# A two-layer encoder trunk: the small matmuls of attention gathered into fewer bursts, weights made ready a unit ahead

## The chip, the cores and the metric

The kernel runs on one core of a Trainium2 chip. The metric is the device time of one execution in microseconds (us); lower is better. Five engines work side by side: TensorE (PE in the profile; its weight loads are PEld), VectorE (DVE), ScalarE (ACT), GpSimd (POOL) and SyncE (SP), which here issues most of the DMA transfers.

## The reference

512 tokens of width 1024 go through two layers, each an attention and a SwiGLU network (width 2816), with RMSNorm ahead of each and at the end. Everything is float32.

```python
for i in range(DEPTH):
    h = rmsnorm(x, norm_mix[i])
    if i % 2 == 0: x = x + window_gqa_sink(h, w_qkv_a[j], w_out_a[j], sink_a[j])
    else:          x = x + dilated_mixture_attention(h, w_qkv_b[j], w_out_b[j])
    x = x + swiglu(rmsnorm(x, norm_ffn[i]), w_gate[i], w_up[i], w_down[i])
return rmsnorm(x, norm_final)
```

Layer 0's attention: 16 query heads of 64, 4 key and value heads, a token sees 128 tokens to each side, with a linear distance bias and a learned sink logit. Layer 1's: three groups of 16 heads, each with queries, keys and values of its own: (window 128, dilation 1), (512, 4), (2048, 16). A dilated group sees only the tokens of its own residue class. The three outputs of a head are merged with weights from the softmax denominators:

```python
for gi, (win, dil) in enumerate(DILATED_GROUPS):
    ...
    o, lse = banded_attention(q, k, v, slopes, dil, win // (2 * dil), BLOCK_B)
wts = jax.nn.softmax(jnp.stack(lses), axis=0)
o = jnp.einsum('gbsh,gbshd->bshd', wts, jnp.stack(outs))
```

## The kernel before

**Projections.** A weight block of 1024x128 is a *unit*: it is loaded (`wraw`, by SyncE), split by ScalarE into a high part `wh` and by VectorE into a low part `wl` (`split`, L93 and L94), and multiplied in three products per 128 rows (`mm3`, L122): high by high, high by low, low by high, each in two matmuls of 256 columns. The buffers for `wraw`, `wh` and `wl` number three each. `unit` is a generator with 8 steps of six matmuls; `values` makes the values of four heads out of two weight blocks in 16 steps of six matmuls. When a unit's last matmul is issued, its `done` is called: for a query or key unit of layer 1 VectorE scales the result out of PSUM (L980, L991).

**The order on TensorE is written by hand**; the other engines' instructions are put in order by a planner. The small matmuls of attention are the main thread and the projection steps are *fillers* between them, so that TensorE has work while ScalarE and VectorE are at the softmax. `spread([a, 3, b], fill)` runs `a`, then three filler steps, then `b`; `weave(steps, fill, total)` spreads `total` filler steps over the steps of a list.

**Layer 1, a pair of heads at a time (8 pairs).** Its parts, with what they are called in the profile:

- `scores_a` (L1036, tile `sc`): scores of group 0, two tiles at a time; VectorE adds the bias and takes the maximum (L1044), ScalarE the exponential (L1049). Queries and keys of group 0 are used in split form: `split_keys` (called in `k_done`) writes the tiles `ks` and `kl` from the key unit's result with four copies on ScalarE for the high parts (L136, L137), two subtractions on VectorE (L138) and two copies of the low parts on ScalarE (L139).
- `merge`: the maxima and denominators of group 0 go by GpSimd's DMAs (L1165, L1166, L1171) through DRAM into another order of tokens (`sa`).
- `turn_a` (L1058, tile `tp`): transposes of the probabilities; `weigh_a` (L1073, L1077, tile `ov`): their products with the values, taken over by ScalarE into `acca` (L1082).
- `scores_b` (L1095): scores of the two dilated groups, for two of four classes at a time; maximum on VectorE (L1108), minimum with group 0's (L1111), exponential on ScalarE (L1115), the sum of all three groups (L1118 to L1120), then the probabilities are scaled on ScalarE (L1127).
- `turn_b` (L1137 on TensorE, L1140 on VectorE): transposes; `merge_rows` (L1177): group 0's weights, multiplied into `acca` (L1179).
- `weigh_b` (L1150, tile `ov`): products with the dilated values, added to `acca` (L1156) and split into `oh`, `ol` (L93, L94).

`scores_b` uses 64 of the 128 rows of TensorE's array per matmul, two matmuls side by side; `weigh_a` and `weigh_b`, like `weigh` of layer 0 (L394), use 64 columns each.

`attention_a` lists the first three of these groups and `attention_b` the last three. The fillers of a pair p are its dilated query and key units, values where they are due, the query and key unit of group 0 for pair p+1, and at the end parts of the output projection (`out_part`).

**Layer 0.** 16 units of attention (four groups of heads by four blocks of 128 queries). Each has scores (L144), softmax on VectorE and ScalarE, scaling on GpSimd (L373), transposes `turn` (L380, evacuated at L384 and L386), and `weigh` (L394), whose result ScalarE and VectorE split into `oh` and `ol` (L398, L399). `weigh` of one unit stands after the first `turn` of the next, and the scores run two units ahead.

PSUM has eight banks: three with the tag `mm`, two `sc`, two `tp`, one `ov`.

Of the kernel before, what the change touches and what calls it, by code (L numbers as in the profile page):

```python
# [16 lines left out]
NK = D // 128  # L17
# [49 lines left out]
def trunk(ctx, tc, xT, gains, sink, tabs, qsc, wunits, wv, outT, outR):  # L67
# [81 lines left out]
    def run(gen):  # L149
        for _ in gen:  # L150
            pass
# [19 lines left out]
                for _ in range(step):  # L171
                    next(fill)

    def unit(u, hi, lo, tag, done, cuts=(0, NK)):


        def gen():
            tiles = weight_tiles()
            wh, wl = chunks(tiles, (NK, 128))
            ps = bank(tag)  # L180
            for j in range(NK):
                if j in cuts:
# [10 lines left out]
    def values(i, col, hi, lo, out, tags="mm mm mm mm"):  # L193


        def gen():
            w = [load_unit(wv[2 * i + k], (4, 256), 96, 1 + (i == 0 and k == 0)) for k in range(2)]
            for b in range(4):
# [112 lines left out]
    with tc.tile_pool(name="l0", bufs=2) as pool:  # L311
# [26 lines left out]
        def attention0(P, h, b):  # L338
# [37 lines left out]
            def turn(kb):  # L376
                tp = bank("tp")
                for hf in range(2):
                    for i in range(2):
                        nc.tensor.transpose(tp[:, 256 * hf + 128 * i:256 * hf + 128 * i + 128],  # L380
                                            st["pr"][:, 2 * i + hf, 128 * kb:128 * kb + 128], ident)
                pt = st["pt", kb] = pool.tile([128, 512], F32, name="pt", bufs=4)
# [5 lines left out]
            def weigh():  # L388

                ov = bank("ov")  # L390
                for kb in range(nb):
                    for hf in range(2):
                        vs = slice(64 * (2 * P + hf), 64 * (2 * P + hf) + 64)
                        nc.tensor.matmul(ov[64 * hf:64 * hf + 64, :256], v0[:, k0 // 128 + kb, vs],  # L394
                                         st["pt", kb][:, 256 * hf:256 * hf + 256], start=(kb == 0),
                                         stop=(kb == nb - 1))
                src = ov[:, :256].rearrange("p (i q) -> p i q", i=2)
                nc.scalar.activation(oh[:, own, block], src, AF.Copy)  # L398
                nc.vector.tensor_tensor(ol[:, own, block], src, oh[:, own, block].bitcast(F32), op=OP.subtract)  # L399

            rest = [lambda kb=kb: turn(kb) for kb in range(nb)]
            return [lambda: scores(0), lambda: scores(1)], rest, weigh


        gens = [k_unit(0, cuts=(0, 2, 4, 8))[1], q_unit(0, 0, cuts=(0, 2, 4, 8))[1], q_unit(0, 1, cuts=(0, 4, 8))[1]]
# [43 lines left out]
        late = None  # L449
        for n, (_, rest, last) in enumerate(units):  # L450
            nexts = units[n + 2][0] if n + 2 < len(units) else []
            steps = []
            for k in range(len(rest)):
                steps += rest[k:k + 1] + nexts[k:k + 1]
                if k == 0 and late:
                    steps.append(late)
            late = last
            if n == len(units) - 1:
                steps.append(late)
            weave(steps, fill, counts[n])  # L460
        for j in range(3):
            run(out_part(j, 6, NK)[1])
# [492 lines left out]
    with tc.tile_pool(name="l1", bufs=2) as pool:  # L955
# [10 lines left out]
        def qk_units(p, g):  # L966
# [28 lines left out]
                    split_keys(k, qk["ks", p], qk["kl", p])  # L995

            at = u1 + 6 * p + 2 * g
            return [unit(at, xh, xl, "mm", q_done), unit(at + 1, xh, xl, "mm", k_done)]

        def v_unit(pg, g):  # L1000
# [3 lines left out]
            vals[pg, g] = v = pool.tile([128, 4, 256], F32, name="v1", bufs=3)  # L1004
            return values(1 + 3 * pg + g, 4, xh, xl, v)

        def evacuate(pt, tp, k):
            if k % 2:
# [43 lines left out]
        def turn_a(p, ts, t):  # L1052
# [7 lines left out]
            pt = st["pt"] = pool.tile([128, 512], F32, name="pt1", bufs=4)  # L1060
            evacuate(pt[:, :2 * n], tp[:, :2 * n], t)
            return pt

# [20 lines left out]
        def scores_b(p, cs):  # L1084


            ps = [bank("sc") for a in range(2)]
            pr = st["pr", p, cs] = pool.tile([128, 2, 512], F32, name="pr1", bufs=2)
            for c in cs:
                cols = slice(128 * c, 128 * c + 128)  # L1090
# [33 lines left out]
                                    den[:, :, :, None].to_broadcast([128, 2, 2, 64]), op=OP.mult)  # L1124
            for c in cs:
                for a in range(2):
                    nc.scalar.activation(of(pr[:, a, :], c), of(pr[:, a, :], c), AF.Copy,  # L1127
                                         scale=den[:, c % 2, a:a + 1])

        def turn_b(p, cs):  # L1130

            pr = st["pr", p, cs]
            pts = [pool.tile([128, 512], F32, name="pt1", bufs=4) for _ in range(2)]
            tp = bank("tp")
            for a in range(2):
                for c in range(2):
# [44 lines left out]
        def attention_a(p):  # L1181
# [14 lines left out]
        def attention_b(p, pauses=(0, 0, 0, 0, 0)):  # L1196
            pts = {}

            def turn(cs):
                pts[cs] = turn_b(p, cs)  # L1200

            def weigh():
                for c in range(4):
                    weigh_b(p, c, pts[c // 2 * 2, c // 2 * 2 + 1])
# [5 lines left out]
        def out_part(j, lo, hi, ps={}, w={}):  # L1210
            def gen():
                if lo == 0:
                    w[j] = load_unit(wunits[u1 + 48 + j], (NK, 128))
                    ps[j] = bank("mm")
                wh, wl = w[j]
                for c in range(lo, hi):
# [11 lines left out]
        for j in range(NK):  # L1228
            operands(2, j, oh, ol)

        for _, gen in (q_first, k_first):
            for _ in range(NK - 1):
                next(gen)
        run(q_first[1])
        norm_sums(True)
        run(k_first[1])
        gens = [v_unit(pg, 0)[1] for pg in range(4)]
        spread([3, lambda: norm_rows(at=4)], gens[0])
        for gen in gens:
            run(gen)  # L1240

        def fillers():
            for p in range(8):
                pg = p // 2
                yield from chain(*qk_units(p, 1), *qk_units(p, 2))
                if p == 0:
                    yield from chain(v_unit(0, 1), v_unit(0, 2))
                elif p % 2 == 0:
# [5 lines left out]
            yield from chain(*[out_part(j, lo, hi) for lo, hi in ((0, 6), (6, 7)) for j in range(3)])  # L1254
# [107 lines left out]
```

## Time and profile before

| | us |
|---|---|
| median of 3 runs | 1414.99 (1414.75 to 1415.15) |
| the profiled execution | 1415.99 |
| its span, first to last instruction | 1414.2 |
| TensorE busy | 1398.6 (99%) |
| TensorE's weight loads | 1373.4 (97%) |
| VectorE busy | 855.3 (60%) |
| ScalarE busy | 706.6 (50%) |
| GpSimd busy | 193.9 (14%) |

A line of the *chain of work that ended last* has a start, a duration, an engine, a tile, a line of the code and the number of instructions (`x6`); times count from the span's start. A line of the *timeline* has a start and a duration, the engine, line and operation, what is written from what, the shape, and in brackets how long the engine had been idle before it and what ended that. A line of the *waits* reads: who waited for whom, us in total, how often, the longest. A line of *busy time by stretch* has the stretch, its length, and the busy time and number of instructions of each engine. Shares of busy time are means over stages that have different limits; TensorE's matmuls are pipelined, so a busy TensorE isn't one at its peak.

### The profile page before, as it was taken

The page shows a single profiled execution, that of the slowest core. Times are in us where ns is not written, and L with a number is a line of the kernel's source. Part 1 is how long each engine was busy: PE and PEld are TensorE (multiplying, and loading weights), DVE is VectorE, ACT ScalarE, POOL GpSimd, SP SyncE. Part 2 cuts the span into 40 slices and gives each one's busy share as a digit, 9 for nine tenths or more (in the row PEclk, how much of TensorE's full clock was granted, in tenths as well). Part 3 has the DMA queues.
Part 4 walks back from the last instruction along what each step waited for, and adds up shares of the span by engine and source line. Part 5 has one row for each costly group of instructions (what it writes and reads, how often), then busy time and mean ns, then how long its engine had stood idle before and what let it go on. Part 6 is the DMA issues. An engine that isn't in the chain of part 4 may idle for free.

```text
span 1414.2 us, 29663 instructions
## 1 busy us (share of the span) xinstructions
PE 1398.6 (99%) x12418; PEld 1373.4 (97%) x12418; DVE 855.3 (60%) x1589; ACT 706.6 (50%) x1319; POOL 193.9 (14%) x261
## 2 busy tenths in 40 slices
PE   8999999999999999999999999999999999999998
PEld 8888999999999999999999999999999999999997
DVE  6777558853787365346546556556465894378633
ACT  6776534632565365445546536546443463256522
POOL 4334230100110020001001000010022010011022
PEclk9999999999999999999999999999999999999999
DMA  6110263743773242312222122222127284388222
GB/s 200 61 46 31 76 180 105 193 129 106 195 196 88 73 131 92 96 60 91 76 76 88 63 91 73 79 76 75 61 91 194 89 210 118 107 203 192 67 95 72
DMA packets 60486, 153.62 MB, mean 109 GB/s; under 512 B 8256, under 2 KB 13632, under 8 KB 60352
## 3 DMA queue, kind: packets, MB, share of 16 engines
q1 hardware_dynamic: 49168, 134.26, 28.7%
q0 software_dynamic: 10752, 16.92, 7.5%
q8 instruction: 97, 1.59, 0.5%
q10 hardware_dynamic: 432, 0.54, 0.1%
q14 instruction: 37, 0.30, 0.1%
HBM read 149.52 MB, written 2.17 MB: 107 GB/s over the span
## 4 chain that ended last, share of the span: by engine, by line
PE 94%; ACT 2%; DVE 2%; issue 1%; DMA 0%; POOL 0%; SPq 0%; DVEq 0%; ACTq 0%
PE mm L122 38%; PE mm L670 12%; PE sc L122 11%; PE psv L122 10%; PE sc L670 9%; PE tp L122 4%; PE sc L1095 1%; PE sc L1036 1%; PE ov L394 1%; PE ov L1150 1%; PE tp L380 1%; PE sc L144 1%; PE tp L1058 1%; PE ov L1077 1%; ACT pr L369 0%
## 5 line engine op out<-in xcount | busy, mean ns | idle before, releaser
L93 ACT ACTIVATE wh<-wraw 128x1024 fp32r<-128x1024 f32 (+4 forms) x192 | 181.1, 948 | 256.0 <-PE mm L122 139.7
L94 DVE TENSOR_TENSOR wl<-wraw,wh 128x1024 fp32r<-128x1024 f32 (+4 forms) x192 | 213.4, 1115 | 150.9 <-ACT wh L93 146.1
L122 PE MATMUL mm<-xh,wh 128*128 128x256 f32 x1320 | 269.7, 284 | 1.3 <-ACT wh L93 1.3
L122 PE MATMUL mm<-xh,wl 128*128 128x256 f32 x1320 | 261.7, 278 | 1.0 <-DVE wl L94 1.0
L122 PE MATMUL mm<-xl,wh 128*128 128x256 f32 x1320 | 261.2, 278 | 0.0
L122 PEld LDWEIGHTS mm<-xh,wh 128*128 128x128 f32 x1320 | 201.7, 189 | 7.1 <-issue 4.8
L122 PEld LDWEIGHTS mm<-xh,wl 128*128 128x128 f32 x1320 | 201.2, 189 | 1.3 <-DVE wl L94 1.2
L122 PEld LDWEIGHTS mm<-xl,wh 128*128 128x128 f32 x1320 | 201.4, 189 | 0.2 <-DVE xl L222 0.2
L627 POOL DMA_DIRECT2D w<-wunits x64 | 56.2, 916 | 419.9 <-DVE wl L650 156.1
L235 POOL TENSOR_TENSOR ssum<-ssum,tmp 128x512 f32<-128x512 f32 x33 | 54.0, 1638 | 211.7 <-ACT tmp L232 114.2
L122 PE MATMUL psv<-wh,xh 128*128 128x256 f32 x288 | 82.4, 286 | 0.0
L122 PE MATMUL psv<-wl,xh 128*128 128x256 f32 x288 | 80.2, 278 | 0.0
L122 PE MATMUL psv<-wh,xl 128*128 128x256 f32 x288 | 80.1, 278 | 0.0
L670 PE MATMUL mm<-bh,wh 128*128 128x256 f32 x256 | 70.7, 276 | 0.0
L670 PE MATMUL mm<-bl,wh 128*128 128x256 f32 x256 | 70.7, 276 | 0.0
L670 PE MATMUL mm<-bh,wl 128*128 128x256 f32 x256 | 70.7, 276 | 0.0
L670 PE MATMUL sc<-bh,wh 128*128 128x256 f32 x256 | 70.7, 276 | 0.0
L670 PE MATMUL sc<-bl,wh 128*128 128x256 f32 x256 | 70.7, 276 | 0.0
L670 PE MATMUL sc<-bh,wl 128*128 128x256 f32 x256 | 70.7, 276 | 0.0
L670 PE MATMUL mm<-bh,h 128*128 128x256 f32 x256 | 70.7, 276 | 0.0
L670 PE MATMUL mm<-bl,h 128*128 128x256 f32 x256 | 70.7, 276 | 0.0
L670 PE MATMUL mm<-bh,l 128*128 128x256 f32 x256 | 70.7, 276 | 0.0
(240 smaller groups left out, 3705.9 us busy)
## 6 DMA issues: line engine op xcount, KB each, us to landing
wraw<-wunits SPq DMA_DIRECT2D x159, 512.0 KB, 3.2
w<-wunits SPq DMA_DIRECT2D x96, 256.0 KB, 5.0
w<-wunits POOLq DMA_DIRECT2D x64, 256.0 KB, 6.0
wraw<-wv SPq DMA_DIRECT2D x25, 512.0 KB, 3.8
wraw<-wunits SPq DMA_DIRECT2D x28, 192.0 KB, 2.4
x<-xT SPq DMA_DIRECT2D x8, 256.0 KB, 4.7
wraw<-wunits SPq DMA_DIRECT2D x4, 256.0 KB, 4.8
wraw<-wunits SPq DMA_DIRECT2D x2, 384.0 KB, 3.0
```

The source lines that it names most:

```text
L93: nc.scalar.activation(out_h, src, AF.Copy)
L94: nc.vector.tensor_tensor(out_l, src, out_h.bitcast(F32), op=OP.subtract)
L122: nc.tensor.matmul(out[:, cols], a, b[:, cols], start=first and k == 0 and c == 0, stop=last and k == 2, skip_group_check=True)
L144: nc.tensor.matmul(outs[a], qp[a][:, qc], k[a][:, kc], start=first and k is kp, stop=k is low, skip_group_check=True)
L235: nc.gpsimd.tensor_tensor(norm["sum"], norm["sum"], sq, op=OP.add)
L380: nc.tensor.transpose(tp[:, 256 * hf + 128 * i:256 * hf + 128 * i + 128], st["pr"][:, 2 * i + hf, 128 * kb:128 * kb + 128], ident)
L394: nc.tensor.matmul(ov[64 * hf:64 * hf + 64, :256], v0[:, k0 // 128 + kb, vs], st["pt", kb][:, 256 * hf:256 * hf + 256], start=(kb == 0), s ...
L627: nc.gpsimd.dma_start(sums[:, 512 * k:512 * k + 512], v[:, 0:512], accum_op=OP.add)
L670: nc.tensor.matmul(out, a[:, j], b[:, j], start=first and j == 0 and i == 0, stop=j == 3 and i == 2, skip_group_check=True)
L1036: nc.tensor.matmul(out, qk["qs", p][a][:, 128 * t:128 * t + 128], kp[k], start=t == ts[0] and k == 0, stop=k == 1, skip_group_check=True)
L1058: nc.tensor.transpose(tp[:, (nb * a + kb) * 128:(nb * a + kb) * 128 + 128], st["pr", p, ts][:, a, o + 128 * kb:o + 128 * kb + 128], ident)
L1077: nc.tensor.matmul(ov[rows, 128 * t - 64:128 * t + 64], v[:, t - 1 + kb, vs], pt[:, 256 * a + 128 * kb:256 * a + 128 * kb + 128], start=Fa ...
```

## The change

In layer 1 the dilated values of a pair (`weigh_b`, now called by `finish`) are multiplied only in the next pair, in front of that pair's `weigh_a`; right behind `weigh_a` both parts of `scores_b` follow, with no filler in between. So `finish(p - 1)`, `weigh_a`, `scores_b(0, 1)` and `scores_b(2, 3)` stand in one piece. The second part of `scores_b` takes the banks `tp`, `finish` a bank `mm` (the last pair: `ov`), and the scaling of the dilated probabilities moves from ScalarE to GpSimd. The fillers' list is made of makers: each unit's weights are loaded and split when the unit before it starts (`lined_up`, `ahead`), and the order in a pair is now group 0's query unit for the next pair, values, then its key unit. In layer 0 `weigh` is done for two blocks at once, in every second unit, into one bank, with one copy and one subtraction of 512 columns. Some buffers grow in number (`pt`, `pt1` 4 to 8, `v1` 3 to 4).

```diff
+    def lined_up(*makers):
+        def first(make):
+            n, gen = make()
+            next(gen)
+            return n, gen
+        following = first(makers[0])
+        for make in (*makers[1:], None):
+            n, gen = following
+            following = make and first(make)
+            for _ in range(n):
+                next(gen)
+                yield
...
             tiles = weight_tiles()
             wh, wl = chunks(tiles, (NK, 128))
+            if ahead:
+                load(tiles, wunits[u], slice(0, 128 * NK))
+                yield
             ps = bank(tag)
...
+        def weigh_two(n):
+            ov = bank("ov")
+            for k in range(2):
+                units[n + k][2](ov, k)
...
+            nc.scalar.activation(hi, src, AF.Copy)
+            nc.vector.tensor_tensor(lo, src, hi.bitcast(F32), op=OP.subtract)
...
-                if k == 0 and late:
-                    steps.append(late)
-            late = last
+                if k == 0 and n and n % 2 == 0:
+                    steps.append(lambda: weigh_two(n - 2))
             if n == len(units) - 1:
-                steps.append(late)
+                steps.append(lambda: weigh_two(n - 1))
...
-            ps = [bank("sc") for a in range(2)]
+            ps = [bank("tp" if cs[0] else "sc", "sc") for a in range(2)]
...
-                    nc.scalar.activation(of(pr[:, a, :], c), of(pr[:, a, :], c), AF.Copy,
-                                         scale=den[:, c % 2, a:a + 1])
+                    nc.gpsimd.tensor_scalar(of(pr[:, a, :], c), of(pr[:, a, :], c), den[:, c % 2, a:a + 1], 1.0,
+                                            op0=OP.mult, op1=OP.mult)
...
-                st["ov"] = bank("ov")
-            ov, hv = st["ov"], 128 * (p % 2)
+                st["ovb"] = bank("ov" if p == 7 else "mm", "ovb")
+            ov, hv = st["ovb"], 128 * (p % 2)
...
             def weigh():
+                if p:
+                    finish(p - 1)
                 for t in range(4):
                     weigh_a(p, t, pts[t])
+                scores_b(p, (0, 1))
+                scores_b(p, (2, 3))
...
-            return [lambda: scores_b(p, (0, 1)), pauses[0], 0, lambda: scores_b(p, (2, 3)), pauses[1], 0, 0,
-                    lambda: turn((0, 1)), pauses[2], 0, 0, lambda: turn((2, 3)), pauses[3], lambda: merge_rows(p),
-                    pauses[4], 0, weigh]
+            return [lambda: turn((0, 1)), lambda: turn((2, 3)), lambda: merge_rows(p)]
+
+        def finish(p):
+            for c in range(4):
+                weigh_b(p, c, st["pts", p, c // 2 * 2])
...
         def fillers():
+            line = []
             for p in range(8):
                 pg = p // 2
-                yield from chain(*qk_units(p, 1), *qk_units(p, 2))
+                v = [lambda pg=pg, g=g, **kw: v_unit(pg, g, **kw) for g in (1, 2)]
+                line += qk_units(p, 1) + qk_units(p, 2)
+                q, k = qk_units(p + 1, 0) if p < 7 else (None, None)
                 if p == 0:
-                    yield from chain(v_unit(0, 1), v_unit(0, 2))
+                    line += [v[0], q, v[1], k]
                 elif p % 2 == 0:
-                    yield from chain(v_unit(pg, 2))
-                if p < 7:
-                    yield from chain(*qk_units(p + 1, 0))
-                    if pg < 3 and p % 2:
-                        yield from chain(v_unit(pg + 1, 1))
...
+                    line += [q, v[1], k]
+                elif p < 7:
+                    line += [q, lambda pg=pg, **kw: v_unit(pg + 1, 1, **kw), k]
...
-        for p in range(7):
+        for p in range(8):
             weave(attention_a(p), fill, 48 if p == 0 else 32)
-            weave(attention_b(p), fill, 32)
-        weave(attention_a(7), fill, 32)
-        spread(attention_b(7, [2, 6, 3, 0, 2]), fill)
+            first, second, rows = attention_b(p)
+            if p < 7:
+                spread([13, first, 8, second, 4, rows, 7], fill)
+        spread([8, first, 5, second, rows, 2, lambda: finish(7)], fill)
         run(fill)
```

More of the change, by code (lines that the diff above doesn't have):

```diff
@@ L172, in spread, with unit @@
                     next(fill)
-    def unit(u, hi, lo, tag, done, cuts=(0, NK)):
+    def lined_up(*makers):
[10 more added lines that the diff above has]
+                yield
+    def unit(u, hi, lo, tag, done, cuts=(0, NK), ahead=False):
         def gen():
@@ L179, in gen @@
             wh, wl = chunks(tiles, (NK, 128))
+            if ahead:
+                load(tiles, wunits[u], slice(0, 128 * NK))
+                yield
             ps = bank(tag)
             for j in range(NK):
-                if j in cuts:
+                if j in cuts and not ahead:
                     load(tiles, wunits[u], slice(128 * j, 128 * cuts[cuts.index(j) + 1]))
@@ L191, in unit, with values @@
         return NK, gen()
-    def values(i, col, hi, lo, out, tags="mm mm mm mm"):
+    def values(i, col, hi, lo, out, tags="mm mm mm mm", ahead=False):
         def gen():
             w = [load_unit(wv[2 * i + k], (4, 256), 96, 1 + (i == 0 and k == 0)) for k in range(2)]
+            if ahead:
+                yield
             for b in range(4):
@@ L386, in turn, with weigh @@
                     nc.scalar.activation(pt, tp, AF.Copy)
-            def weigh():
-                ov = bank("ov")
+            def weigh(ov, n):
                 for kb in range(nb):
@@ L393, in weigh @@
                         vs = slice(64 * (2 * P + hf), 64 * (2 * P + hf) + 64)
[L394 to L399, printed above, removed]
+                        nc.tensor.matmul(ov[64 * hf:64 * hf + 64, 256 * n:256 * n + 256], v0[:, k0 // 128 + kb, vs],
+                                         st["pt", kb][:, 256 * hf:256 * hf + 256], start=(n == 0 and kb == 0),
+                                         stop=(kb == nb - 1), skip_group_check=True)
             rest = [lambda kb=kb: turn(kb) for kb in range(nb)]
             return [lambda: scores(0), lambda: scores(1)], rest, weigh
+        def weigh_two(n):
+            ov = bank("ov")
+            for k in range(2):
+                units[n + k][2](ov, k)
+            P, h, b = n // 8, n // 4 % 2, n % 4
+            own = slice(4 * P + 2 * h, 4 * P + 2 * h + 2)
+            hi, lo = (t[:, own, 128 * b:128 * b + 256].rearrange("p i (b q) -> p b i q", b=2) for t in (oh, ol))
+            src = ov.rearrange("p (b i q) -> p b i q", b=2, i=2)
+            nc.scalar.activation(hi, src, AF.Copy)
+            nc.vector.tensor_tensor(lo, src, hi.bitcast(F32), op=OP.subtract)
         gens = [k_unit(0, cuts=(0, 2, 4, 8))[1], q_unit(0, 0, cuts=(0, 2, 4, 8))[1], q_unit(0, 1, cuts=(0, 4, 8))[1]]
@@ L448, in trunk @@
         spread([10, s0, 1, s1, 1, s2, 1, s3, 2], fill)
-        late = None
-        for n, (_, rest, last) in enumerate(units):
+        for n, (_, rest, _) in enumerate(units):
             nexts = units[n + 2][0] if n + 2 < len(units) else []
@@ L997, in qk_units, with v_unit @@
             at = u1 + 6 * p + 2 * g
-            return [unit(at, xh, xl, "mm", q_done), unit(at + 1, xh, xl, "mm", k_done)]
-        def v_unit(pg, g):
+            return [lambda **kw: unit(at, xh, xl, "mm", q_done, **kw),
+                    lambda **kw: unit(at + 1, xh, xl, "mm", k_done, **kw)]
+        def v_unit(pg, g, **kw):
             if g == 0:
@@ L1003, in v_unit @@
                 return values(1 + 3 * pg, 0, oh, ol, v)
-            vals[pg, g] = v = pool.tile([128, 4, 256], F32, name="v1", bufs=3)
-            return values(1 + 3 * pg + g, 4, xh, xl, v)
+            vals[pg, g] = v = pool.tile([128, 4, 256], F32, name="v1", bufs=4)
+            return values(1 + 3 * pg + g, 4, xh, xl, v, **kw)
         def evacuate(pt, tp, k):
@@ L1059, in turn_a @@
                                         st["pr", p, ts][:, a, o + 128 * kb:o + 128 * kb + 128], ident)
-            pt = st["pt"] = pool.tile([128, 512], F32, name="pt1", bufs=4)
+            pt = st["pt"] = pool.tile([128, 512], F32, name="pt1", bufs=8)
             evacuate(pt[:, :2 * n], tp[:, :2 * n], t)
@@ L1126, in scores_b @@
                 for a in range(2):
-                    nc.scalar.activation(of(pr[:, a, :], c), of(pr[:, a, :], c), AF.Copy,
-                                         scale=den[:, c % 2, a:a + 1])
+                    nc.gpsimd.tensor_scalar(of(pr[:, a, :], c), of(pr[:, a, :], c), den[:, c % 2, a:a + 1], 1.0,
+                                            op0=OP.mult, op1=OP.mult)
         def turn_b(p, cs):
             pr = st["pr", p, cs]
-            pts = [pool.tile([128, 512], F32, name="pt1", bufs=4) for _ in range(2)]
+            pts = [pool.tile([128, 512], F32, name="pt1", bufs=8) for _ in range(2)]
             tp = bank("tp")
@@ L1194, in attention_a, with attention_b, out_part @@
                     lambda: turn((2, 3), 2), 0, lambda: turn((2, 3), 3), 0, 0, weigh]
-        def attention_b(p, pauses=(0, 0, 0, 0, 0)):
-            pts = {}
+        def attention_b(p):
             def turn(cs):
[L1200 to L1204, printed above, removed]
-            return [lambda: scores_b(p, (0, 1)), pauses[0], 0, lambda: scores_b(p, (2, 3)), pauses[1], 0, 0,
-                    lambda: turn((0, 1)), pauses[2], 0, 0, lambda: turn((2, 3)), pauses[3], lambda: merge_rows(p),
-                    pauses[4], 0, weigh]
-        def out_part(j, lo, hi, ps={}, w={}):
+                st["pts", p, cs[0]] = turn_b(p, cs)
+            return [lambda: turn((0, 1)), lambda: turn((2, 3)), lambda: merge_rows(p)]
+        def finish(p):
+            for c in range(4):
+                weigh_b(p, c, st["pts", p, c // 2 * 2])
+        def out_part(j, lo, hi, ps={}, w={}, ahead=False):
             def gen():
                 if lo == 0:
-                    w[j] = load_unit(wunits[u1 + 48 + j], (NK, 128))
+                    for i in range(j, 3 if j == 1 else j + 1):
+                        if i not in w:
+                            w[i] = load_unit(wunits[u1 + 48 + i], (NK, 128))
+                if ahead:
+                    yield
+                if lo == 0:
                     ps[j] = bank("mm")
@@ L1229, in trunk @@
             operands(2, j, oh, ol)
-        for _, gen in (q_first, k_first):
+        gens = [make()[1] for make in (q_first, k_first)]
+        for gen in gens:
             for _ in range(NK - 1):
                 next(gen)
-        run(q_first[1])
+        run(gens[0])
         norm_sums(True)
-        run(k_first[1])
+        run(gens[1])
         gens = [v_unit(pg, 0)[1] for pg in range(4)]
@@ L1242, in fillers @@
         def fillers():
+            line = []
             for p in range(8):
                 pg = p // 2
-                yield from chain(*qk_units(p, 1), *qk_units(p, 2))
+                v = [lambda pg=pg, g=g, **kw: v_unit(pg, g, **kw) for g in (1, 2)]
+                line += qk_units(p, 1) + qk_units(p, 2)
+                q, k = qk_units(p + 1, 0) if p < 7 else (None, None)
                 if p == 0:
-                    yield from chain(v_unit(0, 1), v_unit(0, 2))
+                    line += [v[0], q, v[1], k]
                 elif p % 2 == 0:
-                    yield from chain(v_unit(pg, 2))
-                if p < 7:
-                    yield from chain(*qk_units(p + 1, 0))
-                    if pg < 3 and p % 2:
-                        yield from chain(v_unit(pg + 1, 1))
-            yield from chain(*[out_part(j, lo, hi) for lo, hi in ((0, 6), (6, 7)) for j in range(3)])
+                    line += [q, v[1], k]
+                elif p < 7:
+                    line += [q, lambda pg=pg, **kw: v_unit(pg + 1, 1, **kw), k]
+            line += [lambda j=j, lo=lo, hi=hi, **kw: out_part(j, lo, hi, **kw)
+                     for lo, hi in ((0, 6), (6, 7)) for j in range(3)]
+            return lined_up(*[lambda make=make: make(ahead=True) for make in line])
         fill = fillers()
         spread([4], fill)
-        for p in range(7):
+        for p in range(8):
             weave(attention_a(p), fill, 48 if p == 0 else 32)
-            weave(attention_b(p), fill, 32)
-        weave(attention_a(7), fill, 32)
-        spread(attention_b(7, [2, 6, 3, 0, 2]), fill)
+            first, second, rows = attention_b(p)
+            if p < 7:
+                spread([13, first, 8, second, 4, rows, 7], fill)
+        spread([8, first, 5, second, rows, 2, lambda: finish(7)], fill)
         run(fill)
```

2 lines of the change are left out of this document (1 added, 1 removed).

## The prediction

> **What bounds the kernel now.** I read the page first, then busy time by stretch, then the chain of work in order of time.
>
> ```profile
> PE 94%; ACT 2%; DVE 2%; issue 1%; DMA 0%; POOL 0%; SPq 0%; DVEq 0%; ACTq 0%
> ```
> ```profile
> 31.00:154.00 123.00, 120.25 (x962) 106.34 (x961) 85.19 (x263) 84.13 (x211) 39.96 (x90) 1.00 0.13 45
> 582.00:1034.00 452.00, 451.01 (x4228) 441.26 (x4228) 246.86 (x620) 231.78 (x539) 28.33 (x48) 1.00 0.23 76
> ```
>
> TensorE carries the end. In the attention of layer 1 (582 to 1034 us; busy times in the order TensorE, its weight loads, VectorE, ScalarE, GpSimd) it idles for 1 us of 452, in that of layer 0 for 2.8 us of 123. So nothing large can be won from idle time; what can be won is time in which TensorE is busy at little. The chain shows where that is:
>
> ```profile
> 897.75 1.31 PE ov L1077 x24
> ```
> ```profile
> 929.89 0.91 PE sc L1036 x8
> 930.79 2.72 PE mm L122 x24
> ```
> ```profile
> 957.02 1.09 PE sc L1095 x16
> 958.11 3.62 PE psv L122 x30
> ```
> ```profile
> 977.33 4.11 PE mm L122 x36
> 981.44 1.90 PE ov L1150 x32
> 983.34 1.61 PE mm L122 x12
> 984.95 1.08 PE sc L1036 x8
> ```
>
> An undisturbed projection matmul takes 2.72/24 = 0.113 us. Thirty of them (958.11) between two bursts of dilated scores should take 3.40 us and take 3.62: each burst costs 0.22 us outside itself. Inside it there is a fixed part too: 24 value products that follow others of their kind take 1.31 us, 0.055 each; 32 (L1150) should take 1.75 and take 1.90 (0.15 fixed), 16 scores (L1095) 0.87 and take 1.09 (0.22 fixed). So a burst of half-array matmuls costs 0.37 us (values) or 0.44 us (dilated scores) over its work.
>
> **The change part by part.**
>
> *Fewer bursts, layer 1.* A pair now has four: values of group 0, two of dilated scores, dilated values: 2 x 0.37 + 2 x 0.44 = 1.62 us, 8 pairs 13.0 us. After it there is one per pair, and one more for the last pair's values. One is 0.37 us plus the seam inside it where column halves (128x64, L1077) give way to row halves (64x128, L1095). No row has that seam. Ends: nothing (it can't be a gain, the products' own rate stays) and a whole second burst, 0.44. The nearest row is the scores' own fixed part, 0.22, and I take that. 8 x 0.59 + 0.37 = 5.1: **-7.9 us** (-9.6 to -6.1).
>
> [...]
>
> *Fewer bursts, layer 0.*
>
> ```profile
> 55.47 0.68 PE mm L122 x6
> 56.15 1.01 PE ov L394 x8
> ...
> 65.15 1.45 PE ov L394 x12
> 66.59 0.90 PE mm L122 x6
> ```
>
> Four products more cost 0.44, so 8 cost 0.88 and 0.13 is fixed; the six matmuls behind take 0.90 instead of 0.68, 0.22 more. 0.35 a burst, 16 become 8: **-2.8 us**. The seam between two blocks is within one tiling, so it is free. Against it: even units now hold a double burst and odd ones none, so the scores two units ahead are fed less evenly; 2.8 us of idle is there today, and I add **+0.5** (-0.5 to +2). At the end, as the first row below shows, today one block's copy and subtraction precede the output projection without a gap (321 matmuls in one piece). Now it is two blocks at once, 512 columns, with the same one step (0.68 us) as cover:
>
> ```profile
> 153.50 36.60 PE mm L122 x321
> ```
> ```profile
> 899.11 0.60 ACT L1082 ACTIVATE acca<-ov 128x512 f32<-128x512 f32 x1 [1.50 <-PE ov L1077]
> ```
> ```profile
> 930.09 0.69 DVE L94 TENSOR_TENSOR ol<-tmp,oh 128x512 fp32r<-128x512 f32 x1 [0.70 <-ACT oh L93]
> ```
>
> 0.05 + 0.60 + 0.69 = 1.35 us until the low part is there, wanted at 0.68 + 2 x 0.113 = 0.91: **+0.5** (0 to 0.7).
>
> *What the moved values covered.* This decides. The filler steps (six projection matmuls, 6 x 0.113 = 0.68 us each) are counted in the code: pair 0's line has 80, and 4 + 48 + 32 = 84 are drawn by the start of pair 1; each further pair lists 64 and draws 64. So a pair's line is always finished 4 steps ahead of the next pair's first scores, before and after. The new order ends each pair's line with the key unit of the next pair's group 0 (q, values, k). Its result goes through `split_keys` and is the operand of the next pair's first scores, L1036, 4 steps later. Today the key unit stands last for the even pairs alone, and the burst L1150 lies within these 4 steps: 977.33's piece holds the unit's end and 12 matmuls, then 1.90 us of values, 12 more matmuls, L1036. The engines in that stretch:
>
> ```profile
> 980.12 1.07 DVE L991 TENSOR_TENSOR ka<-mm,rb 128x512 f32<-128x512 f32 x1 [1.35 <-PE mm L122]
> ```
> ```profile
> 979.94 1.06 ACT L93 ACTIVATE wh<-wraw 128x1024 fp32r<-128x1024 f32 x1 [3.68 <-issue]
> 981.22 1.28 ACT L136 ACTIVATE ks<-ka 64x512 fp32r<-64x512 f32 x2 [0.22 <-DVE ka L991]
> 982.53 1.28 ACT L137 ACTIVATE ks<-ks 64x512 fp32r<-64x512 f32 x2
> 983.83 1.29 ACT L139 ACTIVATE kl<-kl 64x512 fp32r<-64x512 f32 x2
> ```
>
> From the key unit's end (12 matmuls before 981.44, 980.08) the six copies on ScalarE are done at 985.12. TensorE came at 984.95 and the eight scores took 1.08 us instead of 0.91: just late, 0.17 us, at four pairs. After the change the values are gone from there: TensorE comes at 980.08 + 2.72 = 982.80, and its fourth score matmul, the first that needs the last copy, is due at 983.14 and can go at 985.15: 2.0 us of standing. No order of the six copies shortens it, since they alone are 3.85 us behind a VectorE step of 1.07, and a weight split put among them adds up to 1.06. It comes at pairs 1 to 7 (pair 0's keys are made long before): 7 x 2.0 - 4 x 0.17 = **+13.3 us** (12 to 20). Behind the waiting scores stand the fillers, so nothing is made up.
>
> *Dilated scores at once, scaling on GpSimd.*
>
> ```profile
> 1013.40 0.42 DVE L1108 CUSTOM_DVE_ANT_0 pr<-sc,tab 128x256 f32<-128x256 f32 x1 [3.63 <-PE sc L1095]
> ```
> ```profile
> 1018.41 1.71 ACT L1127 ACTIVATE pr<-pr,mb 128x256 f32<-128x256 f32 x4 [1.14 <-DVE mb L1120]
> ```
> ```profile
> 142.77 0.94 POOL L373 TENSOR_SCALAR pr<-pr,mst 128x256 f32<-128x256 f32 x2 [0.44 <-DVE mst L371]
> 941.41 2.24 POOL L1171 DMA_DIRECT2D sa<-stats  x4 [2.01 <-DMA stats<-sta]
> ```
>
> From scores to scaling is 5.0 us; four scalings take 1.7 on ScalarE and 4 x 0.47 = 1.9 on GpSimd. The first turn stands 13 steps (8.8 us) behind the burst's end, and its scores end 0.9 earlier still: 9.7 against 6.9. Cost nothing, 2.8 us of cover; with that gone, each us late is a us for TensorE. GpSimd's queue has room: the next pair's statistics come later than the scalings, and the merged maxima (last row) are issued some 9 us ahead of the group's values at 953, so the burst finds them landed. The second scores' banks (`tp`) were emptied 7 steps (4.8 us) earlier, and the dilated keys have a step of 0.68 plus 3.6 us of values for one VectorE operation of 0.69.
>
> *Last pair, weights ahead.*
>
> ```profile
> PE mm L122 <- DVE wl L94: 1.7, 2, 1.0
> ```
> ```profile
> PE tp L1137 <- ACT pr L1127: 1.0, 2, 0.5
> ```
> ```profile
> ACT wh L93 <- PE mm L122: 139.7, 56, 7.1
> ```
> ```profile
> 1028.76 1.06 DVE L1156 TENSOR_TENSOR tmp<-ov,acca 128x512 f32<-128x512 f32 x1 [2.60 <-PE ov L1150]
> 1029.85 0.63 ACT L93 ACTIVATE oh<-tmp 128x512 fp32r<-128x512 f32 x1 [4.23 <-DVE tmp L1156]
> ```
>
> Weights: ScalarE waits for a unit to be finished before it can split into its buffers, so splits already run as far ahead as three buffers let them; TensorE waited twice, 1.7 us, once at the kernel's start. Nothing (-1.0 to +1). In the last pair the first turn has 8 steps (5.4 us) against 6.0: 0.5; the last values have 2 steps (1.4 us) against 1.06 + 0.63 + 0.69 and gaps, 2.5: 1.0; the 1.0 that L1137 waits now goes. **+0.5** (-0.5 to +1.5). More buffers of `pt`, `pt1`, `v1` cost space only.
>
> *Sum:* -7.9 - 2.8 + 0.5 + 0.5 + 13.3 + 0.5 = **+4.1 us**. The execution profiled took 1415.99 us; with that 1420.1. The runs' median is 1414.99, 1.0 lower: **1419.1 us**.
>
> **The rivals.**
>
> *The pace (not slower).*
>
> ```profile
> 902.47 3.73 PE mm L122 x30
> ```
> ```profile
> 1035.06 33.72 PE mm L122 x284
> ```
> ```profile
> L122 PE MATMUL mm<-xh,wl 128*128 128x256 f32 x1320 | 261.7, 278 | 1.0 <-DVE wl L94 1.0
> ```
> ```profile
> L670 PE MATMUL mm<-bh,wh 128*128 128x256 f32 x256 | 70.7, 276 | 0.0
> ```
>
> TensorE has two paces for the same matmul: 284 after 1035 us took 0.1187 each, 321 after 153 us 0.1140. The slow one starts at a burst or a wait and lasts until another; 902.47's thirty (3.73) are at it, 958.11's (3.62) not. The mean of L122, 278 ns against 276, puts it at some 0.004 us on near two fifths of 4800 matmuls: 8 us in all, an estimate. Fewer bursts could remove it, more waits could bring it back; I can't forecast which, so it is no term of the sum. From 1.4 us won it makes "no change", from 7.0 "faster"; all won, 1411. Against it: one burst is left per pair, with 13 steps behind it.
>
> *The keys come in time (faster).* If the scores of pairs 1 to 7 don't wait, the sum is -9.9: 1405.1. It needs the last copy within 3.1 us of the unit's end instead of 5.0, which the rows exclude; only a wrong reading of the order allows it.
>
> *Softmax too late (slower still).* If the chain of both dilated scores is longer by over 2.8 us, every first turn waits as well: 1 us over is 8 us, 1427. [...] For that the scalings would have to take 4.7 us instead of 1.9; the 0.94 for two in layer 0 was taken in a stretch where VectorE was busy for 85 of 123 us.
>
> **How the numbers follow.** Some 0.2% (2.8 us) is what can be told from no change here. Forecast as summed, slower by over that: 0.60, with its own range 1417.8 to 1424 from the bounds of seam, copies and layer 0. Pace or small terms take it back: 0.20 (0.14 within 0.2%, 0.06 faster). Keys in time: 0.10, faster. More waits behind the burst: 0.10, slower, 1424 to 1432. Slower 0.70, same 0.14, faster 0.16. The range 1410 to 1426 leaves out the keys in time and the worst of the waits.
>
> **What would show it.** Right: TensorE waits at L1036 for ScalarE's L139, seven times some 2 us in the stretch of layer 1's attention; bursts of 8 + 24 + 32 + 32 in one piece of the chain; eight L394 bursts; no wait at L1137 but in the last pair. Wrong: no idle time ahead of L1036; a matmul group between bursts dearer than today; idle time at L1137 in every pair; a burst of 96 that takes over 6 us.

## The result, and the profile after

The changed kernel takes 1425.45 us (median of 6 runs, 1423.07 to 1426.65) against 1415.03 before: the ratio is 1.0071 (95% interval 1.0058 to 1.0084), 10 us slower. The profiled execution took 1426.05 us, its span 1424.3.

Line numbers have moved: the scores of group 0 are L1063 (were L1036), the dilated scores L1122 (L1095), the dilated values L1177 (L1150, now tile `ovb`). Busy time by stretch of the changed kernel, the two stretches shown of before; the last three columns are TensorE's granted clock, the DMA share and GB/s:

```profile
31.00:154.00 123.00, 120.48 (x986) 109.44 (x986) 84.66 (x257) 84.12 (x205) 39.70 (x90) 1.00 0.13 45
...
582.00:1034.00 452.00, 441.52 (x4099) 433.96 (x4098) 243.88 (x613) 204.55 (x469) 66.77 (x112) 0.98 0.23 76
```

Layer 0's stretch holds 24 matmuls more than before: it got faster. In layer 1's, TensorE idles for 10.5 us where it idled for 1.0, and its clock, 1.00 before, is 0.98. Who waited, TensorE's waits of the changed kernel (us in total, times, the longest):

```profile
PE sc L1063 <- ACT kl L139: 7.2, 12, 0.9
PE sc L1063 <- ACT ks L137: 3.0, 7, 0.4
```

These two are new; L1137's wait for the scaling (1.0 us) is gone. One of the seven places, in the timeline of the changed kernel, ScalarE and then TensorE:

```profile
759.69 1.29 ACT L136 ACTIVATE ks<-ka 64x512 fp32r<-64x512 f32 x2 [0.27 <-DVE ka L1017]
761.00 1.28 ACT L137 ACTIVATE ks<-ks 64x512 fp32r<-64x512 f32 x2
762.30 1.28 ACT L139 ACTIVATE kl<-kl 64x512 fp32r<-64x512 f32 x2
```
```profile
760.88 0.39 PE L122 MATMUL mm<-xh,wl 128*128 128x256 f32 x2
761.68 0.38 PE L1063 MATMUL sc<-ks,qs 128*128 128x256 f32 x1 [0.41 <-ACT ks L137]
762.99 0.39 PE L1063 MATMUL sc<-kl,qs 128*128 128x256 f32 x1 [0.93 <-ACT kl L139]
763.21 0.28 PE L1063 MATMUL sc<-ks,qs 128*128 128x256 f32 x1
763.64 0.44 PE L1063 MATMUL sc<-kl,qs 128*128 128x256 f32 x1 [0.15 <-ACT kl L139]
...
764.73 0.63 PE L122 MATMUL mm<-xh,wh 128*128 128x256 f32 x2
```

The scores wait for the three pairs of copies, one after the other, as forecast. The last row shows what was not: after the wait two projection matmuls take 0.63 us instead of 0.39. Busy time by stretch of the changed kernel, 3.41 us each, at two of the seven pairs:

```profile
702.39:705.80 3.41, 1.91 (x12) 1.31 (x11) 1.42 (x3) 2.92 (x5) 0.00 (x0) 1.00 0.46 154
705.80:709.21 3.41, 3.41 (x18) 3.41 (x17) 2.20 (x14) 1.10 (x5) 0.00 (x0) 0.50 0.00 0
876.47:879.88 3.41, 2.06 (x16) 1.67 (x14) 2.17 (x3) 3.29 (x6) 0.00 (x0) 1.00 0.41 149
879.88:883.29 3.41, 3.25 (x28) 3.05 (x28) 2.20 (x14) 0.84 (x4) 0.00 (x0) 1.00 0.01 5
```

Behind the first wait the granted clock (third column from the right) is 0.50 for 3.41 us, and 18 matmuls fit where some 30 should (3.41/0.113); behind the second, just as long, the clock stays. Five of the seven waits halve it.

I add up, for every matmul between layer 1's first scores and the second network's first block product, the time from its start to the next start, over what it takes undisturbed (0.113 us; for the bursts and transposes the whole time):

| us | before | after | difference |
|---|---|---|---|
| bursts of half-array matmuls, with the matmul on each side | 52.8 | 45.4 | -7.4 |
| standing at group 0's scores | 0.9 | 16.5 | +15.7 |
| half clock | 0 | 7.8 | +7.8 |
| projection matmuls at the slow pace | 6.4 | 4.0 | -2.4 |
| transposes of the dilated groups (last pair's wait) | 6.7 | 5.8 | -0.9 |
| the rest | | | +0.4 |
| sum | | | +13.2 |

Ahead of that stretch the changed kernel is 2.7 us early (layer 0), behind it 0.4: +10.1 in the span.

### The profile page after: what moved, and what is told of

Its sections match the earlier page's. It is cut to its first block, busy times and chain, and to the rows that moved or that the text cites. A ratio compares the mean times of both kernels' runs of the same rounds, so it can differ in the third digit from the quotient of the medians.

```text
span 1424.3 us, 29674 instructions
## 1 busy us (share of the span) xinstructions
PE 1398.5 (98%) x12418; PEld 1377.5 (97%) x12418; DVE 857.0 (60%) x1581; ACT 683.5 (48%) x1247; POOL 232.0 (16%) x325
## 5 line engine op out<-in xcount | busy, mean ns | idle before, releaser
L94 DVE TENSOR_TENSOR wl<-wraw,wh 128x1024 fp32r<-128x1024 f32 (+4 forms) x192 | 214.2, 1119 | 174.6 <-ACT wh L93 173.1
```

Source lines behind the costliest of these rows:

```text
L94: nc.vector.tensor_tensor(out_l, src, out_h.bitcast(F32), op=OP.subtract)
```

## The experiments

Each kernel was timed beside the kernel before on the same chip; ratios are to that.

**Key unit first.**

```diff
-                    line += [v[0], q, v[1], k]
+                    line += [v[0], q, k, v[1]]
...
-                    line += [q, v[1], k]
+                    line += [q, k, v[1]]
...
-                    line += [q, lambda pg=pg, **kw: v_unit(pg + 1, 1, **kw), k]
+                    line += [q, k, lambda pg=pg, **kw: v_unit(pg + 1, 1, **kw)]
```

> The changed kernel, with the key unit of the next pair's group 0 listed ahead of the values instead of behind them. Theory (the wait for the key copies, and the half clock that follows it, are the whole loss): all seven waits at the first scores and the half-clock windows go, 15.7 us and 7.8 us; the kernel comes out at 1425.5 - 23.5 = 1402 us, 1400 to 1404 with the pace, 0.99 of the kernel before. Rival (the one long burst, or GpSimd's scaling, makes its own waits and pulls the clock down): a few of the windows stay or come at another place, and the time is 1408 or more.

1407.27 us, ratio 0.9937 (0.9924 to 0.9951): 8.9 us faster than before. Its stretch of layer 1:

```profile
582.00:1034.00 452.00, 450.79 (x4281) 446.52 (x4281) 258.01 (x625) 214.36 (x484) 70.38 (x114) 1.00 0.24 77
```

The idle time is 1.2 us, the clock 1.00, no wait at L1063 is left. So the order of the keys is the cause of the loss, and everything else in the change is worth 9 us. It came out 5 us above the forecast; the pace explains most of that, below.

**One step more ahead.**

```diff
-        spread([4], fill)
+        spread([5], fill)
         for p in range(8):
-            weave(attention_a(p), fill, 48 if p == 0 else 32)
+            weave(attention_a(p), fill, {0: 48, 7: 31}.get(p, 32))
```

> The changed kernel with one filler step more drawn at the start of layer 1's attention (5 instead of 4) and one less in pair 7's first part, so that each key unit is finished 5 steps ahead of the first scores and each wait is 0.68 us shorter, some 1.5 us instead of 2.2. Theory (the clock is halved for 3.4 us when over half of the 3.4 us before were idle): no half-clock window is left in the attention of layer 1, so 7 x 0.68 + 7.8 = 12.6 us are won and the time is 1413 us (1411 to 1415). Rival (any wait of over a microsecond can halve the clock): only the waits shrink, 4.8 us, and the time is 1420 to 1421 with four or five half-clock windows.

1416.49 us, ratio 1.0002 (0.9993 to 1.0011), some 10 us better than the changed kernel. The stand at L1063 fell from 16.5 to 11.7 us, by 4.8 as 7 x 0.68 says, and no half-clock stretch is left (clock 1.00 over 582 to 1034 us). The same place as above:

```profile
703.79:707.20 3.41, 2.34 (x19) 1.94 (x18) 1.62 (x3) 3.14 (x5) 0.00 (x0) 1.00 0.44 154
707.20:710.61 3.41, 3.41 (x31) 3.41 (x32) 2.76 (x15) 1.01 (x5) 0.00 (x0) 1.00 0.02 5
```

31 matmuls in the second stretch, at full clock. Both terms went as the theory has them; the time is some 3 us above it. In the profiled execution 1.1 us of that is slow pace in this stretch (5.1 against 4.0), and some 2 us lie ahead of layer 1's first scores (585.0 us against 582.1, of which 0.68 is the added step), where stretches of projection matmuls ran at the slow pace too.

**A busy wait.** TensorE is given products of the identity while it stands anyway.

```diff
+            def stay_busy():
+                if p == 0:
+                    return
+                spare = bank("ov", "spare")
+                for _ in range(16):
+                    nc.tensor.matmul(spare[:, :128], ident, ident, start=True, stop=True)
...
-            return [lambda: scores_a(p, (0, 1)), 0, ...
+            return [lambda: (stay_busy(), scores_a(p, (0, 1))), 0, ...
```

> The changed kernel with 16 products of the identity with itself (128 columns, 0.11 us each, 1.7 us) in front of the first scores of pairs 1 to 7, into a bank that nobody reads: TensorE does them in time in which it stands anyway, and the operands of the scores come no sooner. Theory (the clock falls because TensorE idles over half of a 3.4 us stretch): the half-clock windows go and nothing else changes, 7.8 us won over the changed kernel: some 3 us slower than before instead of 10 (1.5 to 4). Rival (the clock falls for another reason, the long burst or the load's rhythm): the windows stay, and the time stays within 2 us of the changed kernel's.

1430.38 us, ratio 1.0108 (1.0092 to 1.0125). The clock stayed up (1.00 over 582 to 1034 us), but the load was too long: this product is two passes, as TensorE's timeline of this kernel shows.

```profile
762.56 3.73 PE L1229 MATMUL spare<-ident 128*128 128x128 f32 x32
766.05 0.36 PE L1063 MATMUL sc<-ks,qs 128*128 128x256 f32 x1
```

32 instead of 16, 3.5 us where TensorE stands 2.2. As a test of the time it is void. With `range(8)`:

> As the busy wait before, with 8 products of the identity instead of 16. Each turned out to be two passes of 0.109 us, so 16 lasted 3.5 us where TensorE stands 2.2, and added 9 us of their own; 8 last 1.75 us and fit in. Theory (the clock falls for idle time alone): no half-clock window in layer 1's attention, the stand at the scores as long as in the changed kernel, 7 to 8 us won over it in the same session. Rival (something else halves the clock, the 16 only pushed it aside): windows at some pairs, and within 2 us of the changed kernel.

1418.05 us, ratio 1.0023 (1.0014 to 1.0032). Its stretch, with 12 us of useless products in it:

```profile
582.00:1034.00 452.00, 450.85 (x4294) 445.35 (x4292) 245.58 (x614) 205.03 (x470) 66.80 (x112) 1.00 0.23 76
```

The changed kernel beside it on the same chip:

> The changed kernel once more, beside the run above. Theory: four to six half-clock windows of 3.4 us, each behind a stretch of 3.4 us that was idle for over half; 8 to 11 us slower than before, and each run's time goes with its number of windows, some 1.6 us each. Rival: the windows come at places that the idle time doesn't order.

1425.76 us, ratio 1.0080 (1.0067 to 1.0094). Useless work in the wait makes the kernel 7.7 us faster, with the scores' operands no earlier; the sum of the half-clock matmuls was 7.8. That idling is what halves the clock here is shown: over this stretch it is 1.00 with the products in the wait and 0.98 without. The second profile of the changed kernel gives the bound more closely:

```profile
934.93:938.34 3.41, 2.01 (x12) 1.61 (x13) 1.11 (x4) 2.16 (x4) 0.00 (x0) 1.00 0.47 154
938.34:941.75 3.41, 3.41 (x18) 3.41 (x17) 1.74 (x12) 1.86 (x8) 0.57 (x1) 0.50 0.00 0
876.91:880.32 3.41, 2.06 (x15) 1.63 (x14) 2.06 (x3) 3.29 (x6) 0.00 (x0) 1.00 0.41 143
880.32:883.73 3.41, 3.26 (x29) 3.08 (x28) 2.21 (x14) 0.84 (x4) 0.00 (x0) 1.00 0.03 11
```

2.01 us busy of 3.41: halved. 2.06: not. But busy time as the profile gives it doesn't draw the line. On the same grid, near the start of the first profile, lies a stretch that was busy for less, and the clock stayed:

```profile
12.90:16.31 3.41, 1.93 (x17) 1.73 (x16) 3.41 (x3) 3.41 (x7) 3.24 (x4) 1.00 0.34 112
16.31:19.73 3.42, 3.42 (x31) 3.42 (x31) 3.42 (x6) 1.15 (x3) 3.42 (x6) 1.00 0.36 101
```

The number of TensorE's matmuls in a stretch (the figure behind its busy time; all of 256 columns) orders these cases: 12 or 13 ahead of the five halvings of the first profile and of the one shown of the second, 15 or more where the clock stayed. At 0.113 us each, 13 are 1.5 us of the 3.41, and 15 are 1.7, just half; the half that the expectations name is an estimate of mine that goes with these cases, no more. What the chip goes by is not shown. The five halved stretches of the first profile begin at 705.80, 763.83, 821.86, 937.91 and 995.93 us, which is 17, 17, 34 and 17 times 3.413 us apart. The wait at the pair around 877, as long as the others, is cut by a boundary of this grid (879.88), 0.32 us of it beyond, and no halving follows; that the boundary is the reason is likely, not shown. The mean clocks of the six runs (0.992 to 0.995, the two fastest runs with the two highest) fit one halved stretch more or less, and so do the four runs here (the slowest, 1428.69 us, has the lowest clock, 0.990); that is not shown, only likely.

**The burst taken apart again** (on the kernel with the key unit first).

```diff
                 if p:
                     finish(p - 1)
+                next(fill)
                 for t in range(4):
                     weigh_a(p, t, pts[t])
+                next(fill)
                 scores_b(p, (0, 1))
+                next(fill)
                 scores_b(p, (2, 3))
...
-                spread([13, first, 8, second, 4, rows, 7], fill)
-        spread([8, first, 5, second, rows, 2, lambda: finish(7)], fill)
+                spread([10, first, 8, second, 4, rows, 7], fill)
+        spread([5, first, 5, second, rows, 2, lambda: finish(7)], fill)
```

> The kernel with the key unit first, its one burst taken apart again: one filler step between the dilated values, group 0's values, and each of the two parts of the dilated scores (three steps, taken from those behind the burst). Theory (0.37 us for a burst of values, 0.44 for one of scores, 0.2 for the seam in the merged one): 7 x (0.37 + 2 x 0.44 - 0.2) + 0.7 = 8 us slower than with one burst, near the kernel before. Rival (the small matmuls cost the same wherever they stand, and the gain comes from the waits and the pace): within 2 us of the kernel with the key unit first.

1413.16 us, ratio 0.9985 (0.9976 to 0.9994), against 0.9937: by the ratios 6.8 us slower, by the medians 5.9, with the same idle time: near the theory's 8, far from the rival's 2. In the profiled executions the way from layer 1's first scores to the second network's first block product is 7.0 us longer (542.7 against 535.7). One pair in the chain of both kernels, first in one piece, then apart:

```profile
728.19 1.90 PE ovb L1177 x32
730.09 0.23 PE ov L1100 x8
730.32 1.31 PE ov L1104 x24
731.63 1.99 PE sc L1122 x32
```
```profile
726.22 1.90 PE ovb L1177 x32
728.12 0.90 PE mm L122 x6
729.02 0.38 PE ov L1100 x8
729.41 1.31 PE ov L1104 x24
730.72 0.89 PE mm L122 x6
731.61 1.09 PE sc L1122 x16
732.70 0.90 PE mm L122 x6
733.60 1.09 PE sc L1122 x16
```

Six projection matmuls between bursts take 0.90 us instead of 0.68, and a burst that begins anew pays its fixed part (16 scores take 1.09 us, 0.21 over 16 x 0.055). The seam from column halves to row halves can be read off too: 32 scores behind the values take 1.99 us, 0.24 over 32 x 0.055. Forecast 0.22.

**Layer 0 alone** (the kernel before with `weigh_two` and eight buffers for `pt`, as in the change's diff).

> The kernel before with the change of layer 0 alone (values of two blocks at once, pt with 8 buffers). Theory (each burst costs 0.35 us, eight fewer, little given back): 2.5 to 3 us faster, 1412 to 1412.5. Rival (the double copy at the end and the uneven bursts give it back): within 0.5 us of before.

1414.53 us, ratio 0.9987 (0.9978 to 0.9996): 1.8 us faster, 0.6 to 3.1. The sign is clear, the size lies below the forecast's 2.5 but its interval holds it.

**GpSimd's scaling alone** (the kernel before with the `gpsimd` lines of the diff).

> The kernel before with the scaling of the dilated probabilities on GpSimd alone. Theory (hidden, 2.8 us of cover or more in every pair but the last): within 0.7 us of before, the last pair's transposes waiting some 0.3 us longer than today. [...]

1417.12 us, ratio 1.0005 (0.9996 to 1.0014): no difference to tell. But the operation isn't always as cheap as I took it. GpSimd's groups, of this kernel and then of the changed one (mean ns of one behind the busy time):

```profile
L1127 POOL TENSOR_SCALAR pr<-pr,mb 128x256 f32<-128x256 f32 x64 | 51.1, 812 | 184.2 <-DVE mb L1120 108.3 <-ACT wh L93 56.5 <-DVE mb L1111 19.4
```
```profile
L1154 POOL TENSOR_SCALAR pr<-pr,mb 128x256 f32<-128x256 f32 x64 | 38.3, 612 | 156.2 <-DVE mb L1147 153.7 <-ACT wh L93 2.5
```

Means of 0.81 and 0.61 us, where layer 0's row had 0.47. The mean misleads: the shortest, the median and the longest of the changed kernel's 64 (ns), and then four in a row in the timeline, one of them long, with VectorE's instruction beside it:

```profile
L1154 POOL TENSOR_SCALAR pr<-pr,mb x64: 467/476/1442, 623.9 to 1032.9; 128x256 f32<-128x256 f32 x64
```
```profile
741.81 2.94 POOL L1154 TENSOR_SCALAR pr<-pr,mb 128x256 f32<-128x256 f32 x4 [0.42 <-ACT wh L93]
743.03 1.38 DVE L94 TENSOR_TENSOR wl<-wraw,wh 128x1024 fp32r<-128x1024 f32 x1
```

57 take 0.47 to 0.61 us, seven 1.44, and each of the seven runs for 1.1 us beside VectorE's weight split L94, which subtracts one tile in SBUF from another. That the split is the cause is read from what runs side by side, not from an experiment. The four scalings with a long one take 2.94 us instead of 1.9, 1.0 of the cover of 2.8.

**Scaling on ScalarE again** (the kernel with the key unit first).

> The kernel with the key unit first, the dilated probabilities scaled on ScalarE again. Theory (2.8 us of cover at the first turn, 1.7 us of scalings on ScalarE): within 1 us of the kernel with the key unit first; only in the last pair the first turn may wait a little more. Rival (the burst puts 16 us of work on ScalarE, and GpSimd's help is what keeps the turns on time): waits at the turns of most pairs, 3 us slower or more.

1407.05 us, ratio 0.9935 (0.9922 to 0.9948), the same as with GpSimd (0.9937).

**No unit ahead** (the kernel with the key unit first; the fillers' makers run one after the other).

```diff
-            return lined_up(*[lambda make=make: make(ahead=True) for make in line])
+            return chain_made(*line)
...
+        def chain_made(*makers):
+            for make in makers:
+                yield from make()[1]
```

> The kernel with the key unit first, each unit's weights asked for at its own start again (no unit ahead). Theory (the splits run as far ahead as three buffers let them in any case): within 1.5 us of the kernel with the key unit first, no new wait of TensorE for wh or wl. Rival (the burst fills VectorE and ScalarE, and only weights asked for a unit ahead are ready): waits of TensorE at wh and wl behind the bursts, 3 us slower or more.

1406.57 us, ratio 0.9935 (0.9922 to 0.9948): nothing. In this kernel weights a unit ahead neither help nor hurt.

## Why the prediction was right or wrong

Slower was forecast, for the reason found; but 4.1 us were forecast and 10.4 measured. 1425.45 us lies above the range that went with the sum (1417.8 to 1424) and 0.6 us inside the outer one (1410 to 1426), whose upper end was meant for waits behind the burst that did not come. That it lies inside is luck: a term of 7.8 us was missing, and the pace, which had no term either, gave 2.4 back.

- *The wait for the keys.* Place, mechanism and number were right: L1063 behind ScalarE's L139, seven times. Forecast 2.0 us each and 13.3 in all, measured 15.7: each ran some 0.3 us longer. The last copy ends 5.2 us behind the key unit's end and not 5.0. The copies took as long as before (5.0 us from the start of L991, now L1017, to L139's end); the unit's end was read 0.2 us late, because I counted back from the burst at 0.113 us a matmul, and the one just ahead of a burst takes 0.2. And the first score behind the last wait takes 0.22 us instead of 0.11 (880.30 to 880.52 in the first profile, at full clock).
- *The half clock.* This term was missing: 7.8 us, more than the whole error of 6.3. The prediction said that behind the waiting scores stand the fillers, so nothing is made up; it took the fillers behind them at full pace. The two rows of before showed a clock of 1.00, and I took a wait of 2 us for no more than its length.
- *Fewer bursts, layer 1.* Forecast -7.9, measured -7.4; the burst taken apart costs 5.9 to 6.8 us in time. The seam was 0.24 for 0.22.
- *Layer 0.* Forecast -2.8 + 0.5 + 0.5 = -1.8; the trace gave -2.7, the experiment alone -1.8. Between the two blocks of a double burst there is no seam: 20 products take 2.31 us (63.95 to 66.26 in the changed kernel), and 0.13 + 20 x 0.11 is 2.33.
- *Scaling on GpSimd, weights ahead.* Forecast nothing, measured nothing, each undone by itself. GpSimd's 0.47 was the usual price; left out were the seven scalings of 1.44 us beside VectorE's subtractions, and the cover held them.
- *Last pair.* Forecast +0.5. The transposes' wait went (-0.9); where the last values are awaited TensorE now idles for 0.4 us (for `oh` and `ol`).
- *The pace* was a rival without a term. It gave 2.4 us back here. The kernel with the key unit first lost that again (6.4 us at the slow pace, as before the change), and its profiled execution had 1.6 us of it in group 0's values as well and some 1.2 more in layer 0's output projection; that is most of why it missed its own forecast. The two paces side by side, in the chain of the kernel with the key unit first:

```profile
701.78 2.83 PE mm L122 x24
...
709.32 5.66 PE mm L122 x48
...
723.41 4.78 PE mm L122 x42
```

0.118 us each, then 0.114. The prediction has the slow one start at a burst or a wait; in the changed kernel it also starts at 740.42 us, inside a piece of projection matmuls (0.113 us each ahead of it, 0.118 behind). What puts TensorE into one or the other stays open.

The key unit first beats both kernels: 1407.27 us.

## What to carry to other kernels

Before small work is moved away from where it stands, ask what it covered: the values that seemed to be mere overhead were 1.9 us of the 5.0 that the next operands needed. Gathering half-array matmuls into one burst is worth some 0.3 us for each burst saved (7.4 us for 23 in layer 1), on a kernel that TensorE bounds. And price a wait of TensorE not by its length alone: in the first profile of the changed kernel five of seven waits, each with 1.91 to 1.93 us busy in a 3.41 us stretch, were followed by 3.41 us at half clock, another 1.6 us each.

## What the runs showed of the hardware that I had not expected

A wait of some 2.1 us at one pair, in three parts of which none was over 1.2 us, halved TensorE's clock for 3.41 us: with 1.9 to 2.0 us busy in a stretch of the 3.413 us grid in layer 1's attention it was halved, with 2.06 and 2.34 it was not. A stretch with 1.93 near the kernel's start left it whole, and one with 2.07 near the start of the kernel before (4.80 to 8.21 us) was followed by 3.41 us at 0.50, so the exact line stays open. GpSimd's scaling of 128x256 takes 0.47 us, and 1.44 beside VectorE's subtraction of two tiles in SBUF. And idle time can be bought back with useless matmuls: 12 us of them made the kernel 7.7 us faster.
